# Two-block float32 kernel: scalar_tensor_tensor for tensor_tensor, attention band on TensorE, softmax scaling on ScalarE

## The chip, the core and the metric

The kernel runs on one core of a Trainium2 chip. The metric is the device time of one execution in microseconds (us). The engines are TensorE (PE in the profile; PEld is its weight load), VectorE (DVE), ScalarE (ACT), GpSimd (POOL) and SyncE (SP, which issues most loads). Each engine takes its instructions in order and waits at the first one whose input is not there.

## The reference

One sequence of 512 tokens with 1024 features passes two blocks in float32, each of depth 2. The first block mixes retention and a gated linear recurrence and has a gated feed-forward part. In the second block, each of its two layers (l = 0, 1) runs a sliding-window attention and a delta-rule recurrence (rwkv7) side by side, joins them, and has a feed-forward part with a convolution. What the change touches most is the attention, 16 query heads in 4 groups, 4 blocks of 128 queries:

```python
s = jnp.einsum('bnhqgd,...') * 64 ** -0.5
s = jnp.where(mask, s, -jnp.inf)          # band: 0 <= distance < 128
m = jnp.maximum(jnp.max(s, -1, keepdims=True), sink)
pr = jnp.exp(s - m)
pr = pr / (jnp.sum(pr, -1, keepdims=True) + jnp.exp(sink - m))
```

and, in the recurrence, the keys' factor `k = k * (1.0 + (iclr - 1.0) * k_a)`.

## The kernel before

Every large product is made of three fast matmuls (`mm_k`, L303 to L305): weights and activations are each split into a rounded high part and a rest, and high by high, high by rest and rest by high are added in PSUM. The high part is a copy on ScalarE (L287 for weights, L277 for activations), and the rest is a subtraction of two SBUF tiles on VectorE (L288, L278); in the stage below the weights' rest runs on GpSimd instead (`lo_eng`). Other work uses plain float32 matmuls.

`mixer2` is the stage around the change; it occurs once in each of the two layers. Generators for the recurrence's keys (`rw_a`, `rw_solve`) and for the attention (`attention`) are woven together by estimated costs, and the tile framework then orders each engine's instructions. The keys run alone at first (one pair of heads out of four), then beside the attention. From `rw_a` this text needs: `ic` comes from ScalarE, `t` is `ic` times one column plus another (L1141, VectorE), `k` is multiplied by `t` on GpSimd (L1142), `bk` takes products on VectorE (L1146, L1147), and 8 matmuls read `bk` (L1157). `rw_solve` is a chain of 62 small VectorE instructions (L1185, L1186). `rope2` rotates a projection out of PSUM with five VectorE instructions (L943, L946) and one addition on GpSimd (L947).

An attention item is one group and one block of queries: 16 items in a layer, of which 12 see 256 keys (wide) and 4 see 128 (narrow). `att_scores` makes an item's scores: four float32 matmuls with 64 rows (QK, L983) into two PSUM banks, `sc` for the two heads with e = 0 and `mg` for those with e = 1, one buffer each. e = 0 reads partitions 0 to 63 and e = 1 partitions 64 to 127. For each bank VectorE adds the band mask while copying to SBUF (L988) and takes the maximum (L989); three tiny instructions (L991 to L993) bring in the sink; ScalarE takes four exponentials with their sums (L996); VectorE divides (L998, L999) and scales the four heads (L1001). `att_values` transposes the result two items later (L1012, L1014) and multiplies by the values (L1023).

## Time and profile before

| what | us |
|---|---|
| three runs, median (lowest to highest) | 4038.07 (4033.7 to 4040.94) |
| the profiled execution | 4036.65 |
| its span, first to last instruction | 4034.8 |
| TensorE busy in it (modelled ends) | 3762.3 (93%) |
| VectorE busy | 2667.9 (66%) |
| ScalarE busy | 1774.9 (44%) |
| GpSimd busy | 576.6 (14%) |

The profiled execution lies 1.4 us below the median. Matmuls overlap in the pipeline and their ends are modelled, so a share of busy time near 100% does not say that TensorE runs at its peak; how close two matmuls start to each other says more. [...]

### The profile page before, as it was taken

Reading aid. Unit: us, or ns where it says so; the run is one execution under the profiler, and the core shown is the slowest. Engines: PE = TensorE matmul, PEld = TensorE weight load, DVE = VectorE, ACT = ScalarE, POOL = GpSimd, SP = SyncE. Lnnn points to the kernel's source line nnn. Section 1 sums busy time; section 2 is a strip of 40 time slices with the busy share of each in tenths; the row PEclk is TensorE's granted clock in tenths of the full one; section 3 lists DMA queues with packets and bytes.
Section 4 is the critical chain, followed back from the end, with each engine's and each line's share of the span. In section 5 each row is a group of like instructions: output and inputs, shape, how many; then the busy total and the mean of one; then the engine's idle time right before and its main releaser. Section 6 shows DMA issues by size and latency. Waiting matters only on the chain.

```text
span 4034.8 us, 56574 instructions
## 1 busy us (share of the span) xinstructions
PE 3762.3 (93%) x19888; PEld 3117.2 (77%) x19888; DVE 2667.9 (66%) x5595; ACT 1774.9 (44%) x3727; POOL 576.6 (14%) x515
## 2 busy tenths in 40 slices
PE   7998999999999988889999999998888989999998
PEld 6877888888888876657778888896665777888887
DVE  7888444555644567887664676687788775476667
ACT  4433333544433352435553554455344555354444
POOL 0201000110100033222110200014331220020001
PEclk9999999999999998989999999999888999999999
DMA  8466333312333343343227433344334323743334
GB/s 287 153 204 189 97 94 95 94 48 63 100 95 96 91 147 105 97 128 109 91 65 255 124 107 92 99 153 152 96 98 130 110 81 101 234 126 97 94 96 137
DMA packets 316573, 487.34 MB, mean 121 GB/s; under 512 B 79744, under 2 KB 127744, under 8 KB 316160
## 3 DMA queue, kind: packets, MB, share of 16 engines
q1 hardware_dynamic: 240256, 422.82, 34.0%
q10 hardware_dynamic: 76032, 60.90, 4.7%
q8 instruction: 157, 2.57, 0.3%
q14 instruction: 128, 1.05, 0.1%
HBM read 422.72 MB, written 60.88 MB: 120 GB/s over the span
## 4 chain that ended last, share of the span: by engine, by line
PE 55%; DVE 13%; ACT 3%; issue 3%; POOL 1%; DMA 1%; ACTq 0%; SPq 0%; POOLq 0%; DVEq 0%
PE ps L303 15%; PE ps L304 15%; PE ps L305 15%; DVE tm L1185 2%; PE ps L1317 1%; DVE tt L1186 1%; PE ps L1300 1%; PE ps L1157 1%; DVE ro L946 1%; DVE wl L288 1%; PE ps L983 1%; ACT wh L287 1%; PE ps L1023 1%; PE ps L1280 1%; PE ps L1285 1%
## 5 line engine op out<-in xcount | busy, mean ns | idle before, releaser
L303 PE MATMUL ps<-hi,wh 128*128 128x512 f32 (+1 forms) x4384 | 1635.3, 374 | 41.5 <-DVE ro L946 18.1
L305 PE MATMUL ps<-hi,wl 128*128 128x512 f32 (+1 forms) x4384 | 1622.1, 371 | 9.7 <-DVE wl L288 5.2
L304 PE MATMUL ps<-lo,wh 128*128 128x512 f32 (+1 forms) x4384 | 1622.7, 371 | 7.8 <-DVE lo L449 4.6
L287 ACT ACTIVATE wh<-raw 128x512 fp32r<-128x512 f32 (+1 forms) x1158 | 710.1, 620 | 1281.8 <-PE ps L304 1065.7
L288 DVE TENSOR_TENSOR wl<-raw,wh 128x512 fp32r<-128x512 f32 (+1 forms) x1005 | 690.8, 693 | 515.9 <-ACT wh L287 487.1
L303 PEld LDWEIGHTS ps<-hi,wh 128*128 128x128 f32 x4384 | 840.6, 192 | 181.3 <-issue 19.6
L305 PEld LDWEIGHTS ps<-hi,wl 128*128 128x128 f32 x4384 | 841.4, 192 | 143.7 <-DVE wl L288 7.8
L304 PEld LDWEIGHTS ps<-lo,wh 128*128 128x128 f32 x4384 | 842.5, 192 | 138.4 <-DVE lo L449 4.9
L288 POOL TENSOR_TENSOR wl<-raw,wh 128x512 fp32r<-128x512 f32 (+1 forms) x153 | 200.1, 1318 | 1193.2 <-ACT wh L287 1165.2
L1381 POOL TENSOR_TENSOR x<-x,ys 128x256 f32<-128x256 f32 x48 | 43.6, 909 | 862.9 <-DVE ys L1380 793.0
L482 DVE SCALAR_TENSOR_TENSOR ad<-ad,cact 128x1024 f32<-128x1024 f32 x96 | 116.7, 1220 | 29.2 <-DMA ad<-in_ada 29.1
L175 DVE TENSOR_TENSOR acc<-acc,sq 128x256 f32<-128x256 f32 (+1 forms) x175 | 96.1, 552 | 25.2 <-ACT sq L174 23.1
L1157 PE MATMUL ps<-bk,adg 128*128 128x192 f32 x256 | 67.2, 384 | 46.5 <-DVE bk L1147 20.5
L1319 DVE COPY sv<-ps 64x64 f32<-64x64 f32 x224 | 49.5, 221 | 90.4 <-PE ps L1317 87.6
L1185 DVE TENSOR_TENSOR tm<-lu,tt 128x126 f32<-128x126 f32 (+22 forms) x248 | 100.1, 404 | 9.0 <-DMA lu<-ls 4.0
L1580 DVE TENSOR_TENSOR u<-ps,r 128x512 f32<-128x512 f32 x88 | 60.5, 690 | 67.7 <-PE ps L305 67.0
L1317 PEld LDWEIGHTS ps<-sv,add 128*128 128x128 f32 (+1 forms) x512 | 77.9, 189 | 31.9 <-issue 8.8
L1292 POOL TENSOR_SCALAR add<-rdg 64x512 f32<-64x512 f32 x32 | 51.5, 1609 | 351.3 <-DVE add L1301 226.6
L1157 PEld LDWEIGHTS ps<-bk,adg 128*128 128x128 f32 x256 | 47.3, 216 | 64.8 <-issue 34.2
L1317 PE MATMUL ps<-sv,add 128*128 128x64 f32 (+1 forms) x512 | 91.1, 272 | 3.7 <-DVE sv L1319 2.3
L1320 ACT ACTIVATE y<-ps 64x64 f32<-64x64 f32 x256 | 54.7, 216 | 88.7 <-DVE sv L1319 49.5
L1186 DVE TENSOR_TENSOR tt<-tt,tm 128x126 f32<-128x126 f32 (+22 forms) x248 | 80.7, 325 | 3.7
(356 smaller groups left out, 5168.7 us busy)
## 6 DMA issues: line engine op xcount, KB each, us to landing
raw<-in_q_win SPq DMA_DIRECT2D x224, 256.0 KB, 2.9
ad<-in_ada SPq DMA_DIRECT2D x96, 512.0 KB, 4.4
raw<-in_q_w_up SPq DMA_DIRECT2D x184, 256.0 KB, 2.7
raw<-in_win SPq DMA_DIRECT2D x98, 256.0 KB, 3.1
raw<-in_w_val SPq DMA_DIRECT2D x92, 256.0 KB, 2.6
raw<-in_w_gate SPq DMA_DIRECT2D x92, 256.0 KB, 2.8
raw<-in_q_w_down SPq DMA_DIRECT2D x74, 256.0 KB, 2.6
raw<-in_w_down SPq DMA_DIRECT2D x64, 256.0 KB, 2.6
```

What stands on the lines that cost most here:

```text
L175: nc.vector.tensor_tensor(out=self.acc[:, cs], in0=self.acc[:, cs], in1=q, op=ADD)
L287: nc.scalar.activation(h, raw, AF.Copy)
L288: self.lo_eng.tensor_tensor(out=l, in0=raw, in1=h.bitcast(F32), op=SUB)
L303: nc.tensor.matmul(o, h, ah, start=k == first, stop=False)
L304: nc.tensor.matmul(o, h, al, start=False, stop=False)
L305: nc.tensor.matmul(o, l, ah, start=False, stop=k == last)
L482: nc.vector.scalar_tensor_tensor(out=raw, in0=raw, scalar=1.0, in1=self.cact, op0=MUL, op1=MUL, accum_out=m)
L1157: nc.tensor.matmul(o, ad[:, c], bk[:, c], start=True, stop=True)
L1185: nc.vector.tensor_tensor(out=t, in0=lc, in1=tt[:, 0:c, j:j + 1].to_broadcast([P, c, n]), op=MUL)
L1186: nc.vector.tensor_tensor(out=tt[:, 0:c, j + 1:32], in0=tt[:, 0:c, j + 1:32], in1=t, op=ADD)
L1317: nc.tensor.matmul(o, add[h][rows, c], c3(sv[h])[rows, c], start=True, stop=True)
L1580: nc.vector.tensor_tensor(out=u, in0=pj(ff), in1=r2, op=MUL)
```

## The change

1. In about twenty places, a `tensor_tensor` on VectorE with both inputs in SBUF becomes a `scalar_tensor_tensor` that first multiplies by the constant 1.0. Shapes, operands and engine stay. Places on GpSimd and places that read PSUM keep their form.
2. In `att_scores` the mask is no longer added on VectorE. Each QK matmul is preceded by one of identity (128 rows) by band into the same PSUM region, and accumulates on top. The maximum is read from PSUM, the exponentials read PSUM and write the SBUF tile, and the tiny instructions go from three to two.
3. The four scalings of an item move from VectorE to ScalarE.
4. In `rw_a`, `t` moves from VectorE to ScalarE.
5. Once per layer, band and identity are rounded into the matmul's format and the negated sinks are made (three small VectorE instructions).

```diff
@@ weights
-        self.lo_eng.tensor_tensor(out=l, in0=raw, in1=h.bitcast(F32), op=SUB)
+        if self.lo_eng is nc.vector:
+            nc.vector.scalar_tensor_tensor(out=l, in0=raw, scalar=1.0, in1=h.bitcast(F32), op0=MUL, op1=SUB)
+        else:
+            nc.gpsimd.tensor_tensor(out=l, in0=raw, in1=h.bitcast(F32), op=SUB)
...
@@ rope_tables
-        self.band = self.at.tile([P, 256], F32, name=self.name("band"), tag="band")
-        nc.sync.dma_start(self.band, self.I["band"])
+        t = self.T("bd")[:, :256]
+        nc.sync.dma_start(t, self.I["band"])
+        self.band = self.at.tile([P, 256], F32R, name=self.name("band"), tag="band")
+        nc.vector.tensor_copy(self.band, t)
+        self.identr = self.at.tile([P, P], F32R, name=self.name("identr"), tag="identr")
+        nc.vector.tensor_copy(self.identr, self.ident)
...
@@ att_scores
-                hs = slice(64 * e, 64 * e + 64)
-                nc.tensor.matmul(p[:, j * 256:j * 256 + nk], qs[j][hs, n * P:n * P + P], self.kd[g][hs, k0:k0 + nk], start=True, stop=True)
+                hs, o = slice(64 * e, 64 * e + 64), p[:, j * 256:j * 256 + nk]
+                nc.tensor.matmul(o, self.identr, self.band[:, 256 - nk:256], start=True, stop=False)
+                nc.tensor.matmul(o, qs[j][hs, n * P:n * P + P], self.kd[g][hs, k0:k0 + nk], start=False, stop=True)
         for e, p in enumerate(ps):
-            t = self.at.tile([P, S], F32, name=self.name("sc"), tag="sc", bufs=5)
-            v2 = lambda a: a.rearrange("p (e k) -> p e k", e=2)[:, :, 0:nk]
-            bd = self.band[:, 256 - nk:256].rearrange("p (o k) -> p o k", o=1).to_broadcast([P, 2, nk])
-            nc.vector.tensor_tensor(out=v2(t), in0=v2(p), in1=bd, op=ADD)
-            nc.vector.tensor_reduce(out=mx[:, e:4:2], in_=v2(t), axis=AX.X, op=MAX)
-            sc.append(t)
-        nc.vector.tensor_tensor(out=mx, in0=mx, in1=sink, op=MAX)
-        nc.vector.tensor_scalar(out=nm, in0=mx, scalar1=-1.0, scalar2=None, op0=MUL)
-        nc.vector.tensor_tensor(out=es, in0=sink, in1=mx, op=SUB)
+            nc.vector.tensor_reduce(out=mx[:, e:4:2], in_=v2(p), axis=AX.X, op=MAX)
+            sc.append(self.at.tile([P, S], F32, name=self.name("sc"), tag="sc", bufs=5))
+        nc.vector.scalar_tensor_tensor(out=nm, in0=mx, scalar=-1.0, in1=self.nsink[:, 4 * g:4 * g + 4], op0=MUL, op1=ALU.min)
+        nc.vector.scalar_tensor_tensor(out=es, in0=sink, scalar=1.0, in1=nm, op0=MUL, op1=ADD)
...
         for hd in range(4):
-            nc.scalar.activation(view(hd), view(hd), AF.Exp, bias=nm[:, hd:hd + 1], accum_out=sm[:, hd:hd + 1])
+            nc.scalar.activation(view(hd), ps[hd % 2][:, (hd // 2) * 256:(hd // 2) * 256 + nk], AF.Exp, bias=nm[:, hd:hd + 1], accum_out=sm[:, hd:hd + 1])
...
         for hd in range(4):
-            nc.vector.tensor_scalar(out=view(hd), in0=view(hd), scalar1=sm[:, hd:hd + 1], scalar2=None, op0=MUL)
+            nc.scalar.activation(view(hd), view(hd), AF.Copy, scale=sm[:, hd:hd + 1])
...
@@ rw_a
-        nc.vector.tensor_scalar(out=t, in0=ic, scalar1=self.hka[l][:, i:i + 1], scalar2=self.oka[l][:, i:i + 1], op0=MUL, op1=ADD)
+        nc.scalar.activation(t, ic, AF.Identity, bias=self.oka[l][:, i:i + 1], scale=self.hka[l][:, i:i + 1])
...
@@ rw_solve
-            nc.vector.tensor_tensor(out=t, in0=lc, in1=tt[:, 0:c, j:j + 1].to_broadcast([P, c, n]), op=MUL)
-            nc.vector.tensor_tensor(out=tt[:, 0:c, j + 1:32], in0=tt[:, 0:c, j + 1:32], in1=t, op=ADD)
+            nc.vector.scalar_tensor_tensor(out=t, in0=lc, scalar=1.0, in1=tt[:, 0:c, j:j + 1].to_broadcast([P, c, n]), op0=MUL, op1=MUL)
+            nc.vector.scalar_tensor_tensor(out=tt[:, 0:c, j + 1:32], in0=tt[:, 0:c, j + 1:32], scalar=1.0, in1=t, op0=MUL, op1=ADD)
```

Outside `mixer2` the order of every engine is the same before and after. Inside it the framework orders anew. Lines of the changed kernel stand some 10 to 17 lower in its file: QK is L1001 there, the band's matmul L1000, the exponential L1009, the scaling L1014, `t` L1154, the projections L313 to L315.

TensorE, first layer, the first wide item (`ps_13959` is its bank `sc`, `ps_13960` its bank `mg`, `kd` the keys, `ro` the rotated queries; L1157 and L305 are the keys' and a projection's matmuls). Before:

```order
6791 L983 MATMUL ps_13959<-kd_13594,ro_13747 128x256
6792 L983 MATMUL ps_13960<-kd_13594,ro_13747 128x256
6793 L983 MATMUL ps_13959<-kd_13594,ro_13792 128x256
6794 L983 MATMUL ps_13960<-kd_13594,ro_13792 128x256
6795 L1157 MATMUL ps_14034<-bk_13139,adg 128x192
```

And in the changed kernel:

```order
6791 L1000 MATMUL ps_13966<-band_13528,identr_13530 128x256
6792 L1001 MATMUL ps_13966<-kd_13600,ro_13753 128x256
6793 L1000 MATMUL ps_13967<-band_13528,identr_13530 128x256
6794 L1001 MATMUL ps_13967<-kd_13600,ro_13753 128x256
6795 L1000 MATMUL ps_13966<-band_13528,identr_13530 128x256
6796 L1001 MATMUL ps_13966<-kd_13600,ro_13798 128x256
6797 L1000 MATMUL ps_13967<-band_13528,identr_13530 128x256
6798 L1001 MATMUL ps_13967<-kd_13600,ro_13798 128x256
```

Two QK matmuls on different partitions no longer stand next to each other; a matmul of 128 rows stands between any two.

ScalarE, the same item: exponentials, a weight's high part (`wh`), and what follows. Before:

```order
1101 L996 ACTIVATE sc_13965,am_13956<-sc_13965,am_13957 128x256
1102 L996 ACTIVATE sc_13968,am_13956<-sc_13968,am_13957 128x256
1103 L996 ACTIVATE sc_13965,am_13956<-sc_13965,am_13957 128x256
1104 L996 ACTIVATE sc_13968,am_13956<-sc_13968,am_13957 128x256
1105 L997 ACTIVATE am_13958<-am_13958 128x4
1106 L287 ACTIVATE wh_14272<-raw_14271 128x512
```

And in the changed kernel:

```order
1108 L1009 ACTIVATE sc_13977,am_13963<-ps_13966,am_13964 128x256
1109 L1009 ACTIVATE sc_13979,am_13963<-ps_13967,am_13964 128x256
1110 L1009 ACTIVATE sc_13977,am_13963<-ps_13966,am_13964 128x256
1111 L1009 ACTIVATE sc_13979,am_13963<-ps_13967,am_13964 128x256
1112 L1010 ACTIVATE am_13965<-am_13965 128x4
1113 L294 ACTIVATE wh_14265<-raw_14264 128x512
1114 L1014 ACTIVATE sc_13977<-sc_13977,am_13963 128x256
1115 L1014 ACTIVATE sc_13979<-sc_13979,am_13963 128x256
1116 L1014 ACTIVATE sc_13977<-sc_13977,am_13963 128x256
1117 L1014 ACTIVATE sc_13979<-sc_13979,am_13963 128x256
1118 L294 ACTIVATE wh_14283<-raw_14282 128x512
```

The exponentials now read the banks, and four scalings stand ahead of the next weight's high part.

TensorE at the third head's keys in the first layer, shortly before the attention's first item (L1133 gives the keys' norms, L1157 needs `bk`, L303 to L305 are projections). Before:

```order
6718 L1133 MATMUL ps_13934<-c_hsel,sq_13841 128x64 x4
6719 L1157 MATMUL ps_14029<-bk_13139,adg 128x192
6720 L303 MATMUL ps_14085<-hi_12302,wh_14105 128x512
6721 L304 MATMUL ps_14085<-lo_12303,wh_14105 128x512
6722 L305 MATMUL ps_14085<-hi_12302,wl_14106 128x512
6723 L303 MATMUL ps_13755<-hi_12288,wh_13757 128x512
```

And in the changed kernel (L1146 is the norms, L1170 the matmul that needs `bk`):

```order
6718 L1146 MATMUL ps_13941<-c_hsel,sq_13848 128x64 x4
6719 L315 MATMUL ps_14095<-hi_12300,wl_14116 128x512
6720 L313 MATMUL ps_14095<-hi_12302,wh_14115 128x512
6721 L314 MATMUL ps_14095<-lo_12303,wh_14115 128x512
6722 L315 MATMUL ps_14095<-hi_12302,wl_14116 128x512
6723 L313 MATMUL ps_13761<-hi_12288,wh_13763 128x512
...
6750 L1000 MATMUL ps_13811<-band_13528,identr_13530 128x128
6751 L1170 MATMUL ps_14038<-bk_13139,adg 128x192
```

The first matmul that needs `bk` stands behind a whole projection now, not ahead of it.

## Rows read from the trace of the kernel before

**Rows 1.** the page's parts 1 and 2: busy us (share of the span) xinstructions; 40 slices

```profile
PE 3762.3 (93%) x19888; PEld 3117.2 (77%) x19888; DVE 2667.9 (66%) x5595; ACT 1774.9 (44%) x3727; POOL 576.6 (14%) x515
DVE  7888444555644567887664676687788775476667
PEclk9999999999999998989999999999888999999999
```

**Rows 2.** by stretch: us, PE, PEld, DVE, ACT, POOL busy (x), clock, DMA, GB/s

```profile
1445.00:1586.00 141.00, 112.15 (x607) 93.39 (x606) 93.28 (x201) 53.94 (x99) 61.12 (x52) 0.93 0.44 137
1586.00:1692.00 106.00, 96.35 (x466) 69.13 (x464) 85.17 (x237) 43.84 (x138) 33.39 (x28) 0.92 0.30 90
1692.00:1798.00 106.00, 88.91 (x409) 60.65 (x407) 88.16 (x265) 42.76 (x127) 17.08 (x14) 0.86 0.34 101
2989.00:3095.00 106.00, 88.98 (x409) 60.72 (x407) 88.40 (x264) 42.46 (x126) 16.97 (x14) 0.86 0.34 101
```

**Rows 3.** groups, VectorE, 1586 to 1798: xcount, busy us, mean ns, idle before

```profile
L988 DVE TENSOR_TENSOR sc<-ps,band 128x512 f32<-128x512 f32 (+1 forms) x32 | 19.6, 617 | 5.2 <-PE ps L1012 3.5 <-PE ps L983 1.5
L1001 DVE TENSOR_SCALAR sc<-sc,am 128x256 f32<-128x256 f32 (+1 forms) x64 | 19.5, 343 | 0.1
L1141 DVE TENSOR_SCALAR t<-ic,om,om 128x512 f32<-128x512 f32 x5 | 5.6, 1113 | 0.0
```

**Rows 4.** in order of time, TensorE: start us, us, instructions in a row

```profile
1725.85 1.05 PE L983 MATMUL ps<-kd,ro 64*128 64x128 f32 x8
1726.83 0.92 PE L1157 MATMUL ps<-bk,adg 128*128 128x192 f32 x4
...
1736.61 1.13 PE L983 MATMUL ps<-kd,ro 64*128 64x256 f32 x8
1737.67 0.50 PE L304 MATMUL ps<-lo,wh 128*128 128x512 f32 x1
...
1738.24 0.40 PE L303 MATMUL ps<-hi,wh 128*128 128x512 f32 x1
1738.57 1.13 PE L983 MATMUL ps<-kd,ro 64*128 64x256 f32 x4
1739.62 0.50 PE L304 MATMUL ps<-lo,wh 128*128 128x512 f32 x1
1739.96 0.40 PE L305 MATMUL ps<-hi,wl 128*128 128x512 f32 x1
1740.20 0.40 PE L303 MATMUL ps<-hi,wh 128*128 128x512 f32 x1
```

**Rows 5.** groups, ScalarE, 1586 to 1798

```profile
L996 ACT ACTIVATE sc<-sc,am 128x256 f32<-128x256 f32 (+1 forms) x64 | 30.0, 470 | 21.3 <-DVE am L992 20.5 <-issue 0.8
```

**Rows 6.** the chain that ended last, 1692 to 1798, shares by line

```profile
by line: DVE tm L1185 10.2%; DVE tt L1186 8.4%; PE ps L1023 7.6%; PE ps L1157 7.4%; PE ps L983 7.1%; PE ps L1012 5.5%; DVE ro L946 5.2%; DVE sc L988 3.8%; DVE am L989 3.4%; PE ps L1121 3.0%; issue 2.8%; DVE x L1158 2.6%; PE ps L304 2.6%; PE
```

**Rows 7.** in order of time, 1565 to 1580: TensorE, then VectorE

```profile
1571.73 0.98 PE L1157 MATMUL ps<-bk,adg 128*128 128x192 f32 x2 [5.33 <-DVE bk L1147]
1578.75 0.77 PE L303 MATMUL ps<-hi,wh 128*128 128x512 f32 x1 [4.76 <-DVE ro L946]
1566.52 0.54 DVE L1141 TENSOR_SCALAR t<-ic,om,om 128x512 f32<-128x512 f32 x1
1570.91 0.68 DVE L1147 TENSOR_TENSOR bk<-zs,wi 128x512 f32<-128x512 f32 x1
1572.86 0.68 DVE L943 TENSOR_TENSOR ro<-ps,cos 128x512 f32<-128x512 f32 x1
```

**Rows 8.** groups by shape, VectorE, whole span

```profile
L288 DVE TENSOR_TENSOR wl<-raw,wh 128x512 fp32r<-128x512 f32 x924 | 646.7, 706 | 508.0 <-ACT wh L287 479.2 <-PE ps L304 12.7 <-DMA raw<-in_q_win 4.1
L1583 DVE TENSOR_TENSOR cv<-cv,cv 128x512 f32<-128x512 f32 x44 | 30.4, 690 | 1.2
```

**Rows 9.** single lines, VectorE: duration ns min/median/max, first and last start

```profile
L1146 DVE SCALAR_TENSOR_TENSOR bk<-ic,wi x16: 635/684/1742, 1515.3 to 3083.8; 128x512 f32<-128x512 f32 x16
L1147 DVE TENSOR_TENSOR bk<-zs,wi x16: 636/678/1761, 1513.0 to 3084.7; 128x512 f32<-128x512 f32 x16
```

More of the change, by code (lines that the diff above doesn't have):

```diff
@@ L269, in load_const, with add_to @@
         return t
+    def add_to(self, pool, out, a, b, op):
+        nc = self.nc
+        if pool:
+            nc.gpsimd.tensor_tensor(out=out, in0=a, in1=b, op=op)
+        else:
+            nc.vector.scalar_tensor_tensor(out=out, in0=a, scalar=1.0, in1=b, op0=MUL, op1=op)
     def split(self, src, T=None):
@@ L277, in split @@
         nc.scalar.activation(h, src, AF.Copy)
-        nc.vector.tensor_tensor(out=l, in0=src, in1=h.bitcast(F32), op=SUB)
+        nc.vector.scalar_tensor_tensor(out=l, in0=src, scalar=1.0, in1=h.bitcast(F32), op0=MUL, op1=SUB)
         return h, l
@@ L448, in put_split @@
             nc.scalar.activation(h, t, AF.Copy)
[L449 removed]
+            self.add_to(k % 2, l, t, h.bitcast(F32), SUB)
         else:
@@ L1332, in rw_seq @@
         rs = self.rsqrt(vr)
-        nc.vector.tensor_tensor(out=c3(y), in0=c3(y), in1=b8(rs), op=MUL)
+        nc.vector.scalar_tensor_tensor(out=c3(y), in0=c3(y), scalar=1.0, in1=b8(rs), op0=MUL, op1=MUL)
         yield 0.0, 6.0
@@ L1634, in evac @@
             y = ys[m][:, cs]
-            nc.vector.tensor_tensor(out=y, in0=y, in1=g, op=MUL)
+            nc.vector.scalar_tensor_tensor(out=y, in0=y, scalar=1.0, in1=g, op0=MUL, op1=MUL)
             n1.add(y, cs)
```

25 lines of the change are left out of this document (14 added, 11 removed).

## Prediction

> **What bounds the kernel now.** The page comes first: over the span TensorE is busy 93%, VectorE 66%, ScalarE 44%, and VectorE's slices lie at 7 or more in the places where TensorE's granted clock dips under 9 tenths [rows 1]. So most of the kernel is bound by TensorE, and work taken from VectorE there is worth nothing. The exception is the stage `mixer2`, which occurs twice; the second time its stretches read like the first within 1 us. Second view, the stretches [rows 2]. 1586 to 1692 (call it B) and 1692 to 1798 (C) hold the 16 attention items of layer 0: nine in B (six wide, three narrow), seven in C (six wide, one narrow). In B TensorE is busy 96 of 106 us and VectorE 85; in C both are at 88 or 89. Neither engine alone is the bound; they hand work to each other and lose time both ways. TensorE loses twice: it idles 9.7 us in B and 17.1 in C, and it runs partly at the lower level, which at a mean granted clock of 0.92 and 0.86 is worth 8.5 us in B and 15 in C. Counted at the full clock its work is therefore 88 us in B and 74 in C. Third view, the chain in C: the largest shares are VectorE's solve chain and TensorE's attention and key matmuls, none over about a tenth [rows 6]. 1445 to 1586 (A) is the keys alone; its end is paced by VectorE [rows 2, 7].
>
> I sum against the profiled execution, 4036.65 us, which is 1.4 below the median of the three runs. About 0.2%, 8 us, is what a measurement here can tell from no change.
>
> **Part 1, the form of the instruction.** The nearest rows for a two-input instruction in SBUF with 512 columns are 690 ns as a tensor_tensor [rows 8] and, on one tile and next to each other, a median of 684 as a scalar_tensor_tensor with a constant and 678 as a tensor_tensor [rows 9]. Between 12 ns saved and 6 ns lost on each of the 924 weights' rests is 11 us of VectorE time to the good or 6 to the bad, and nearly all of them lie where TensorE is the bound. I take 0, and keep a few us for the range.
>
> **Part 2, what VectorE loses.** Per layer, in B and C: 32 additions of the band, 19.6 us, 64 scalings, 19.5, and five `t`, 5.6 [rows 3]. Spread over the items that is about 25 us in B and 19 in C, so VectorE falls from 85 to 60 and from 88 to 69. The maximum reads PSUM now; the band's addition did so too at 617 ns on average [rows 3], so it keeps its price. The three small instructions per layer of part 5 of the change are under 2 us together and stand beside projections.
>
> **Part 3, what TensorE gains.** Four QK matmuls of a wide item that alternate between the two halves of the partitions take 1736.61 to 1737.67, 1.06 us; two of one half alone take 1738.57 to 1739.62, 1.05 us: neighbours on different halves run at the same time, and the same work unpaired takes twice as long [rows 4]. Around the lone two, the projections are late as well: from L303 at 1738.24 to L305 at 1739.96 are 1.72 us, of which two projections at 0.24 (the next step, to 1740.20) are 0.48. So two QK cost 1.24, of which some 0.19 is the way in and out of the 64-row form. If as much again hides inside the 1.05, one bare QK is 0.43. With the band's matmul (256 columns, half of 0.24) between any two, none runs beside another, and each QK pays its own way in and out: 4 x (0.43 + 0.19 to 0.38 + 0.12) is 3.0 to 3.7, and I take 3.5, since the isolated pair is the nearest row. Before, an item costs 1.25 where it stands paired and 2.5 where its banks come free apart; in the order before, about half stand each way, so 1.9. A narrow item goes from 1.2 (0.98 as a row, plus the way in) to 2.6 by the same steps. Per layer: 12 x 1.6 + 4 x 1.4 = 25 us more for TensorE, 14 in B and 11 in C. Without any cost of switching it would be 12 x 0.3 = 4; if all had been paired before, 12 x 2.4 + 4 x 1.7 = 36.
>
> [...]
>
> **Part 4, what ScalarE gains.** 64 scalings per layer; the nearest row is the exponential of the same tiles, 470 ns, so 30 us, and five `t` at under 1 us each [rows 5]. ScalarE goes from 44 to about 61 in B and from 43 to about 59 in C [rows 2]. That is covered by 40 us of idle time in each, unless its order holds something up: the scalings wait for VectorE's reciprocal, and behind them stand weights' high parts, which GpSimd and then TensorE wait for. I cost it at 0; without that cover, one VectorE instruction's wait of 0.7 us per item would be 11 us a layer.
>
> **Part 5, the end of A.** TensorE waits 5.33 us for `bk`, runs three projections, and waits 4.76 us for a rotation to give its bank back [rows 7]. In the new order the matmul that needs `bk` stands a projection later, so the first wait goes; but the rotation begins only at 1572.86 behind `t` (0.54) and `bk` (0.68), and that bank is what is late next. `t` leaves VectorE and L1147 moves behind the rotation, and some POOL conflict with them: I take 3 us, between 1 (the two instructions) and 10 (both waits).
>
> **The sum.** TensorE's work at full clock becomes 88 + 14 = 102 in B and 74 + 11 = 85 in C. What it loses in B (9.7 + 8.5 = 18) and C (17 + 15 = 32) comes mostly from waiting on VectorE. With VectorE's share down by a quarter, I keep half: 102 + 9 = 111 in B (5 longer than 106) and 85 + 16 = 101 in C (5 shorter). With A, 3 us less per layer, 6 in all: 4036.65 - 6 = 4031 us. That is no change that can be told, a little on the fast side.
>
> **Rivals.**
> *VectorE was the pace.* If only a quarter of the losses stays, B is 106.5 and C 93, and with A each layer gains 15.5 us: 4036.65 - 31 = 4006. For it: C's chain, where VectorE's lines hold the first places [rows 6], and both waits of [rows 7]. Against it: B, where TensorE is at 96 of 106. 0.26.
>
> *The banks are held too long* (slower). Before, a bank comes free after one addition on VectorE of 617 ns [rows 3]; after, only when the exponentials have read it: two maxima, the small ones, and three or four exponentials at 470, about 4 us after the last QK. There is one buffer per bank, so the next item's QK waits in TensorE's order, and with it everything behind. It decides where fewer than about 4 us of other matmuls stand between two items; in the new order that is so for some six items per layer, in C above all. At 2.6 us (the four exponentials and their sums' reads) that is 12 x 2.6 = 31 us: 4031 + 31 = 4062. For it: ScalarE already sat idle 20.5 us for the sinks' result ahead of the exponentials [rows 5]. Against it: 16 items share 212 us, 13 each. 0.27.
>
> *TensorE gains the work and gives nothing back.* All losses stay: B 120, C 117, with A 22 us per layer: 4081. Against it: the losses are waits on an engine that gets lighter. 0.08.
>
> *The new form escapes GpSimd.* Held up by GpSimd, a tensor_tensor takes up to 1761 ns, and the weights' rests average 706 where an undisturbed group has 690 [rows 8, 9]. If the new form were never held, 924 x 16 ns = 15 us come off VectorE: 4031 - 15 = 4016 at best. Against it: the scalar_tensor_tensor with a constant took up to 1742 in the same place [rows 9]. 0.03. [...]
>
> **How the numbers follow.** The forecast itself has 0.36. Its own spread, from TensorE's 4 to 36 us per layer and A's 1 to 10, is about 12 us to each side of 4031: 4019 to 4043. Two fifths of that lie more than 8 us under 4036.65, and nothing more than 8 above it. Faster by over 0.2%: 0.26 + 0.03 + 0.4 x 0.36 = 0.43. Within: 0.6 x 0.36 = 0.22. Slower: 0.27 + 0.08 = 0.35. The range reaches from 4002, the first rival with a few us more, to 4064, the banks with a few more; it leaves out the 0.08 and the ends of the others.
>
> **What the profile of the changed kernel would show.** Part 1: the weights' rests at 690 to 710 ns on average. Part 2: VectorE near 60 and 69 us in the two stretches. Part 3: from one QK to the next in an item 0.7 to 0.95 us, and the attention's matmuls no longer in pairs; below 0.6 the lower end holds. Part 4: ScalarE near 60 us per stretch, and little idle time ahead of L1014. Part 5: the wait ahead of the first L1170 of the third head gone. The bank rival would show as TensorE idle ahead of L1000 or L1001 with the exponential, L1009, as what ended it. Wrong altogether would be a change outside the two `mixer2` stages.

## The result and the profile after

The changed kernel took 4091.13 us (median of four runs, 4089.23 to 4093.79) where the kernel before took 4038.59 (four runs): a ratio of 1.0129, 95% interval 1.0116 to 1.0142, so 52 us more. The forecast was 4031 with a range up to 4064. It missed, and on the other side.

The first view is the page again, parts 1 and 2, in the form of [rows 1]:

```profile
PE 3826.8 (94%) x20016; PEld 3157.1 (77%) x20016; DVE 2612.5 (64%) x5361; ACT 1829.3 (45%) x3871; POOL 577.9 (14%) x515
DVE  7888444564644566657664676686666766476667
PEclk9999999999999998989999999998898999999999
```

VectorE lost 55 us of work, ScalarE gained 54, TensorE is busy 64.5 us longer. VectorE's slices fell where `mixer2` runs; the dips of the clock did not go with them.

Where in the program is the time? ScalarE rounds each weights' panel (L287, L294 after), 1158 times in both kernels and in the same sequence, so the k-th of them is a mark in both traces. The 451st stands 1.2 us later after the change, the 571st 31.1, the 811th 30.1, the 946th 55.0, and from there to the end the distance changes by about 1 us. So the loss is made in the two pieces from 451 to 571 and from 811 to 946, the two `mixer2` stages. I divide each at the first score matmul (L983 before, L1001 after) and the last value matmul (L1023, L1036): the keys alone, the attention's stretch, and what follows. First before, then after, in the columns of [rows 2], layer 0:

```profile
1438.00:1586.50 148.50, 119.65 (x642) 99.45 (x640) 100.75 (x218) 58.24 (x110) 67.00 (x58) 0.93 0.45 140
1586.50:1784.10 197.60, 175.12 (x827) 122.38 (x826) 165.70 (x475) 85.32 (x261) 49.60 (x42) 0.88 0.30 91
1784.10:2164.30 380.20, 347.40 (x2003) 277.59 (x2000) 249.32 (x567) 184.48 (x462) 66.19 (x52) 0.98 0.39 123
```

```profile
1439.20:1590.90 151.70, 119.21 (x642) 99.65 (x640) 103.07 (x214) 60.58 (x113) 65.21 (x58) 0.91 0.44 137
1590.90:1808.50 217.60, 201.41 (x884) 136.63 (x883) 134.09 (x368) 109.30 (x328) 49.53 (x42) 0.89 0.27 80
1808.50:2195.40 386.90, 354.94 (x2010) 284.32 (x2007) 253.05 (x561) 185.66 (x465) 67.75 (x52) 0.96 0.38 122
```

How to read them: length less PE busy is TensorE's idle time. The clock column is the mean of TensorE's granted clock as a share of full speed; the records of the two traces, before and after, give it as 1.0 or 0.5 and nothing between, and from one projection of 512 columns to the next are 0.227 us (median) at 1.0 and 0.427 at 0.5, in both. PE busy times (1 - clock) is therefore an estimate of what the lower level cost (the clock is printed to two places, so this is good to about 1 us in the middle row and 2 in the last). In the attention's stretch of layer 0 TensorE's idle time fell only from 22.5 to 16.2 us, its losses to the clock stayed (21.0 and 22.2), and its work at full clock rose by 25. That is 20 us longer, although VectorE has 31.6 us less to do there. Keys alone: 3.2 longer. Behind: 6.7 longer, about what the clock's loss grew by (0.98 to 0.96, 7 us). In the second layer the three are 7.6, 14.2 and 3.2 longer. Over both stages, with the clock unrounded, the changed kernel is 54.8 us longer: TensorE's work at full clock is 46.9 more, its loss to the clock 16.1 more and its idle time 8.2 less.

What TensorE does for the scores, in order of time, as in [rows 4]:

```profile
1644.43 0.40 PE L315 MATMUL ps<-hi,wl 128*128 128x512 f32 x1
1644.66 0.28 PE L1000 MATMUL ps<-band,identr 128*128 128x256 f32 x1
1644.88 0.70 PE L1001 MATMUL ps<-kd,ro 64*128 64x256 f32 x2
1645.50 0.38 PE L1000 MATMUL ps<-band,identr 128*128 128x256 f32 x1
1645.81 0.70 PE L1001 MATMUL ps<-kd,ro 64*128 64x256 f32 x2
1646.44 0.38 PE L1000 MATMUL ps<-band,identr 128*128 128x256 f32 x1
...
1648.32 0.65 PE L1036 MATMUL ps<-pt,vt 128*64 128x256 f32 x4
```

From start to start, a band matmul inside the group takes 0.31 us and a score 0.63 (one score leaves two records, hence x2). The item takes 1644.66 to 1648.32, 3.66 us. Summed over a layer and taken from start to start, idle time left out, the score and band matmuls take 58.0 us of TensorE where the scores took 27.5.

TensorE's waits in layer 0 (1439 to 2195; us in total, times, longest) and two groups of ScalarE's and one of VectorE's in the attention's stretch (the counterparts of [rows 3] and [rows 5]):

```profile
PE ps L313 <- DVE ro L960: 17.6, 4, 12.1
PE ps L1170 <- DVE bk L1159: 10.3, 3, 5.9
PE ps L1000 <- ACT sc L1009: 4.0, 2, 2.0
PE ps L1170 <- DVE bk L1160: 1.3, 2, 1.0
```

```profile
L1014 ACT ACTIVATE sc<-sc,am 128x256 f32<-128x256 f32 (+1 forms) x64 | 25.8, 473 | 20.5 <-DVE am L1012 20.5
L1154 ACT ACTIVATE t<-ic,om,om 128x512 f32<-128x512 f32 x5 | 4.1, 815 | 4.5 <-DMA od<-ao 4.5
L1003 DVE TENSOR_REDUCE am<-ps 128x2 f32<-128x512 f32 (+1 forms) x32 | 19.6, 620 | 26.1 <-PE ps L1001 25.8
```

TensorE waits for the banks (L1000, ended by the exponential L1009) only 4 us. ScalarE stands 20.5 us in front of the scalings for VectorE's reciprocal, where I had expected little. VectorE now sits idle 26 us in front of the maxima for TensorE's scores: there it has become the engine that waits.

### The profile page after: what moved, and what is told of

The parts are those of the page before. It is cut to its first block, busy times and chain, and to the rows that moved or that the text cites. A ratio compares the mean times of both kernels' runs of the same rounds, so it can differ in the third digit from the quotient of the medians.

```text
span 4089.3 us, 56798 instructions
## 1 busy us (share of the span) xinstructions
PE 3826.8 (94%) x20016; PEld 3157.1 (77%) x20016; DVE 2612.5 (64%) x5361; ACT 1829.3 (45%) x3871; POOL 577.9 (14%) x515
## 5 line engine op out<-in xcount | busy, mean ns | idle before, releaser
L313 PE MATMUL ps<-hi,wh 128*128 128x512 f32 (+1 forms) x4384 | 1636.4, 375 | 49.7 <-DVE ro L960 33.2
L315 PE MATMUL ps<-hi,wl 128*128 128x512 f32 (+1 forms) x4384 | 1626.7, 372 | 10.7 <-DVE wl L296 5.8
L294 ACT ACTIVATE wh<-raw 128x512 fp32r<-128x512 f32 (+1 forms) x1158 | 708.8, 620 | 1257.8 <-PE ps L314 1030.9
L296 DVE SCALAR_TENSOR_TENSOR wl<-raw,wh 128x512 fp32r<-128x512 f32 (+1 forms) x1005 | 689.6, 692 | 505.5 <-ACT wh L294 478.6
L313 PEld LDWEIGHTS ps<-hi,wh 128*128 128x128 f32 x4384 | 843.7, 193 | 187.2 <-issue 34.5
L315 PEld LDWEIGHTS ps<-hi,wl 128*128 128x128 f32 x4384 | 841.6, 192 | 147.0 <-POOL wl L298 9.2
L1198 DVE SCALAR_TENSOR_TENSOR tm<-lu,tt 128x126 f32<-128x126 f32 (+22 forms) x248 | 101.9, 411 | 12.7 <-DMA lu<-ls 5.1
L175 DVE SCALAR_TENSOR_TENSOR acc<-acc,sq 128x256 f32<-128x256 f32 (+1 forms) x175 | 95.3, 548 | 22.5 <-ACT sq L174 20.4
L1009 ACT ACTIVATE sc<-ps,am 128x256 f32<-128x256 f32 (+1 forms) x128 | 55.5, 445 | 79.8 <-DVE am L1005 76.3
L1170 PE MATMUL ps<-bk,adg 128*128 128x192 f32 x256 | 68.4, 382 | 24.2 <-DVE bk L1159 19.3
L1199 DVE SCALAR_TENSOR_TENSOR tt<-tt,tm 128x126 f32<-128x126 f32 (+22 forms) x248 | 85.1, 343 | 5.5
```

The source lines that it names most:

```text
L175: nc.vector.scalar_tensor_tensor(out=self.acc[:, cs], in0=self.acc[:, cs], scalar=1.0, in1=q, op0=MUL, op1=ADD)
L294: nc.scalar.activation(h, raw, AF.Copy)
L296: nc.vector.scalar_tensor_tensor(out=l, in0=raw, scalar=1.0, in1=h.bitcast(F32), op0=MUL, op1=SUB)
L313: nc.tensor.matmul(o, h, ah, start=k == first, stop=False)
L315: nc.tensor.matmul(o, l, ah, start=False, stop=k == last)
L1170: nc.tensor.matmul(o, ad[:, c], bk[:, c], start=True, stop=True)
```

## The experiments

All runs stand in one table: median, difference to the kernel before on the same chip, 95% interval of the ratio, and by how much the three stretches of the profiled execution (both layers together) are longer than in that of the kernel before (keys alone 296.5 us, attention 395.1, behind 806.7). The difference is of medians and the ratio of means; the profiled execution can lie some us off its median (e2's 7 below it, e12's 6 above). The order in which each engine's instructions stand is made anew for every kernel, and no run held it fixed; so a difference of some 10 us in one stretch may be the order alone. The runs tell apart what is larger, or what comes back in both layers.

| run | median us | difference | ratio, interval | keys | attention | behind |
|---|---|---|---|---|---|---|
| the change | 4091.1 | +52.5 | 1.0116 to 1.0142 | +10.8 | +34.1 | +9.9 |
| e1 change, band on VectorE | 4064.1 | +27.1 | 1.0051 to 1.0084 | +10.0 | +27.5 | -6.9 |
| e2 band on TensorE alone | 4068.1 | +31.0 | 1.0057 to 1.0102 | +3.2 | +7.9 | +19.4 |
| e3 scalings and t on ScalarE alone | 4067.7 | +30.7 | 1.0060 to 1.0090 | +9.1 | +22.8 | -7.0 |
| e4 form of the instruction alone | 4035.8 | -1.3 | 0.9987 to 1.0006 | +2.9 | -2.1 | -0.7 |
| e5 t alone | 4042.7 | +5.9 | 1.0007 to 1.0026 | +9.4 | +4.5 | -3.6 |
| e6 scalings alone | 4056.0 | +19.2 | 1.0037 to 1.0067 | +1.1 | +25.5 | -9.9 |
| e7 change, bands first | 4044.3 | +7.5 | 1.0010 to 1.0030 | +4.3 | +0.9 | +1.6 |
| e8 band alone, bands first | 4039.2 | +2.4 | 0.9999 to 1.0018 | -0.5 | -0.4 | +2.4 |
| e9 as e6, constant factor | 4052.7 | +15.0 | 1.0020 to 1.0046 | +7.9 | +17.4 | -5.6 |
| e10 as e2, scores in pairs | 4042.8 | +5.0 | 1.0007 to 1.0027 | +0.2 | +11.8 | -4.9 |
| e11 as e2, no band at all | 4024.3 | -13.4 | 0.9948 to 0.9977 | -0.4 | -7.8 | -7.4 |
| e12 loose ScalarE work | 4047.2 | +10.4 | 1.0015 to 1.0034 | +16.3 | -2.3 | -0.2 |
| e13 fused add and maximum | 4030.9 | -5.9 | 0.9977 to 1.0009 | +0.1 | -13.1 | +2.3 |
| e14 two scalings of four | 4044.1 | +7.3 | 1.0004 to 1.0023 | +2.8 | +10.1 | -8.2 |
| e15 tied ScalarE work | 4068.2 | +29.4 | 1.0060 to 1.0089 | +3.0 | +31.1 | -1.2 |
| e16 as e13, minimum | 4047.9 | +9.1 | 1.0015 to 1.0035 | +0.8 | -2.0 | +15.5 |
| e17 e13 again | 4035.5 | -3.4 | 0.9990 to 1.0015 | +2.7 | -5.6 | +0.2 |

### The change in its parts: e1 to e6

The first theory (T): TensorE's added time is the whole loss, and VectorE's relief is worth nothing.

e1, the changed kernel with the band's addition put back to VectorE (maximum and Exp from SBUF and the three small operations come back with it; the lines here are the band's alone):

```diff
-                nc.tensor.matmul(o, self.identr, self.band[:, 256 - nk:256], start=True, stop=False)
+            nc.vector.tensor_tensor(out=v2(t), in0=v2(p), in1=bd, op=ADD)
```

> The changed kernel with the band added by VectorE as before (all its other parts kept). Theory T (TensorE's occupied time goes straight to the end: the score lines take 39.0 + 19.5 us of it per layer where they took 27.5, and the work taken off VectorE gave back 3.5 us of idle): without the band all of the loss goes, 4028 to 4042 us. Rival S (the four scalings, now on ScalarE, lengthen each item): 4055 to 4075. Rival V (the work taken off VectorE is worth what I forecast, some 14 us a layer, and the band hid it): 4005 to 4025.

e2, the kernel before with that one part of the change (maximum and Exp from PSUM and the two small operations come with it; the lines here are the band's alone):

```diff
+                nc.tensor.matmul(o, self.identr, self.band[:, 256 - nk:256], start=True, stop=False)
-            nc.vector.tensor_tensor(out=v2(t), in0=v2(p), in1=bd, op=ADD)
```

> The kernel before with the band on TensorE alone (scalings, the factor t and tensor_tensor stay on VectorE as before). T: 4085 to 4105, the whole loss or more. S: 4055 to 4075, a part of the loss. V: 4060 to 4080, since VectorE's relief of 1.2 us an item would show here too.

e3, the kernel before with

```diff
-            nc.vector.tensor_scalar(out=view(hd), in0=view(hd), scalar1=sm[:, hd:hd + 1], ...
+            nc.scalar.activation(view(hd), view(hd), AF.Copy, scale=sm[:, hd:hd + 1])
-        nc.vector.tensor_scalar(out=t, in0=ic, scalar1=self.hka[l][:, i:i + 1], ...
+        nc.scalar.activation(t, ic, AF.Identity, bias=self.oka[l][:, i:i + 1], scale=self.hka[l][:, i:i + 1])
```

> The kernel before with the four scalings of an item and the factor t on ScalarE alone. T: 4028 to 4042. S: 4050 to 4070. V: 4010 to 4028, as VectorE is relieved of 12 us a layer.

e4, the kernel before with `scalar_tensor_tensor` by 1.0 for `tensor_tensor` in the places of the change, such as

```diff
-        nc.vector.tensor_tensor(out=l, in0=src, in1=h.bitcast(F32), op=SUB)
+        nc.vector.scalar_tensor_tensor(out=l, in0=src, scalar=1.0, in1=h.bitcast(F32), op0=MUL, op1=SUB)
```

> The kernel before with tensor_tensor as scalar_tensor_tensor in VectorE's some twenty places alone. T, S, V: all 4034 to 4042, nothing; if the form takes longer beside GpSimd it would be 4045 or more.

T fell at once, and of the three theories S alone stayed within its bounds in all of e1, e2 and e3. The form costs nothing (e4, as all expected). But the band alone makes only 31 of the 52 us (e2), and without it 27 stay (e1), which is what the two moves to ScalarE cost by themselves (e3, 30.7). Both halves of the change lose about the same. e5 and e6 split the second half: e5 has e3's second pair of lines alone, e6 its first.

> The kernel before with only the keys' factor t on ScalarE. Theory Q (ScalarE's queue stands still in front of each item's scalings, 27.5 us a layer for VectorE's reciprocal, and the copies that TensorE waits for stand behind): t has little part in it, 4040 to 4048 (the keys' stage alone grew by 3 us a layer). Rival K (t itself lengthens the keys' chain, since it takes 815 ns on ScalarE and waits its turn there): 4055 to 4068, the whole of the 31 us.

> The kernel before with only the four scalings of an item on ScalarE. Q: 4055 to 4065, the larger part of the 31 us. K: 4035 to 4045, nothing.

t costs 6, the scalings 19: the scalings are the larger part. And t sits in the keys' stretch (+9.4 in both layers together), the scalings in the attention's (+25.5, of which 9.9 are less work left behind).

Where the band's 31 us lie surprised me. The three stretches of e2, layer 0:

```profile
1434.40:1584.70 150.30, 122.05 (x646) 101.29 (x644) 103.61 (x222) 59.14 (x110) 65.94 (x58) 0.92 0.43 139
1584.70:1782.90 198.20, 188.74 (x881) 131.08 (x882) 149.76 (x430) 81.82 (x258) 47.81 (x39) 0.94 0.29 89
1782.90:2173.10 390.20, 357.53 (x2009) 284.85 (x2006) 253.15 (x562) 186.48 (x465) 70.38 (x54) 0.96 0.37 120
```

In layer 0 the attention's stretch is as long as before (198.2 against 197.6). TensorE works 23 us more at full clock, and its idle time (22.5 to 9.5) and its losses to the clock (21.0 to 11.3) give back just that: 43.5 to 20.8, half, as I had assumed. In the second layer less comes back (43.5 to 26), and the stretch is 7.2 longer. Most of the loss is behind the attention: 10 us longer in layer 0, 9 in the second. One thing to be seen there is that the keys, which share TensorE with the attention, fell behind although the attention did not. The last step of the last solve, in VectorE's order of time, before and in e2:

```profile
1844.98 0.58 DVE L1186 TENSOR_TENSOR tt<-tt,tm 128x16 f32<-128x16 f32 x1
```

```profile
1866.00 0.18 DVE L1189 TENSOR_TENSOR tt<-tt,tm 128x16 f32<-128x16 f32 x1
```

It ends 20.6 us later, and what follows in the stage is built on it. By itself that need not cost: from the attention's end to the end of this step are 61 us before, 83 in e2 and 76 in e15 (below), and e15's third stretch is no longer than before. The other is the clock: 15.8 of the 19.4 us behind the attention, both layers together, are its loss. In one place of e2 it falls:

```profile
1842.00:1862.00 20.00, 17.31 (x69) 14.01 (x68) 12.94 (x40) 4.15 (x10) 0.13 (x1) 0.66 0.41 139
```

With levels of 1.0 and 0.5, a mean of 0.66 is the lower one for two thirds of these 20 us (from 1849 to 1855 the clock was 0.50). TensorE had idled 2.7 us (1842.5 to 1845.2) as this stretch began.

### What the band costs on TensorE: e7, e8, e10, e11

e7 is the changed kernel, e8 the kernel of e2, with

```diff
+        for e, p in enumerate(ps):
+            bd = self.band[:, 256 - nk:256].rearrange("p (o k) -> p o k", o=1).to_broadcast([P, 2, nk])
+            nc.tensor.matmul(v2(p), self.identr, bd, start=True, stop=False)
         for j in range(2):
             for e, p in enumerate(ps):
-                nc.tensor.matmul(o, self.identr, self.band[:, 256 - nk:256], start=True, stop=False)
-                nc.tensor.matmul(o, qs[j][hs, n * P:n * P + P], self.kd[g][hs, k0:k0 + nk], start=False, stop=True)
+                nc.tensor.matmul(o, qs[j][hs, n * P:n * P + P], self.kd[g][hs, k0:k0 + nk], start=False, stop=j == 1)
```

> The changed kernel with one band matmul per bank (both halves at once) ahead of the item's four scores, which follow one another as before. Theory T (the score lines' TensorE time goes to the end as far as the attention's stretch is TensorE's): they fall from 58.5 to some 38 us a layer, so 20 us a layer less at most: 4050 to 4075. Rival (with the scalings on ScalarE the stretch waits for those, and the time saved turns to idle): 4080 to 4092.

> The kernel before with the band on TensorE alone, one matmul per bank ahead of the four scores; scalings and t stay on VectorE. T: up to 20 us a layer less than with the band between the scores (4068): 4025 to 4045. Rival P (in that kernel the attention's stretch was no longer than before, and the loss lies behind it, 8 us a layer of half clock and 3 us of TensorE's work in the stage that follows): the gain in the stretch is small and the loss behind it stays, 4050 to 4068.

e7's loss is 45 us less than the change's, e8's 29 less than e2's: e7 below T's bounds, e8 inside them. The same sums are formed in another sequence, with two band matmuls of 512 columns for four of 256, and 45 of the change's 52 us go: the largest single effect of these runs. TensorE's order of time in e7:

```profile
1601.52 0.61 PE L999 MATMUL ps<-band,identr 128*128 128x512 f32 x2
1602.07 1.14 PE L1003 MATMUL ps<-kd,ro 64*128 64x256 f32 x8
1603.13 0.92 PE L1172 MATMUL ps<-bk,adg 128*128 128x192 f32 x4
```

Both bands take 0.55 us, the four scores 1.06: 1.61 for what took 3.66. Per layer the score and band matmuls take 31.8 us in e7 and 37.7 in e8 (27.5 before). e10 keeps four band matmuls and only pairs the scores (both bands of a half, then both scores; `os2` holds the half's regions in the two banks):

```diff
         for j in range(2):
+            for o in os2:
+                nc.tensor.matmul(o, self.identr, self.band[:, 256 - nk:256], start=True, stop=False)
             for e, o in enumerate(os2):
-                nc.tensor.matmul(o, self.identr, self.band[:, 256 - nk:256], start=True, stop=False)
```

> The kernel before with the band on TensorE alone, four band matmuls as in the change, but both of a half's bands first and then both of its scores, so that two scores follow one another on different halves of the rows. Theory A (what costs is that no two scores are neighbours): the score lines fall from 54 to some 42 us a layer, 4042 to 4052. Rival M (each band matmul and each change of form costs): 4058 to 4068, as with the bands between the scores.

```profile
1649.51 0.53 PE L990 MATMUL ps<-band,identr 128*128 128x256 f32 x2
1649.97 0.70 PE L993 MATMUL ps<-kd,ro 64*128 64x256 f32 x4
1650.61 1.08 PE L1028 MATMUL ps<-pt,vt 128*64 128x256 f32 x8
```

Two neighbours on different halves of the rows take 0.64 us, one alone 0.63 (in the change): the second costs nothing that shows. By the kernel's time theory A holds: 26 of e2's 31 us go when the scores are neighbours again. By the place it is less plain. Of the 27 us a layer that the score and band matmuls take more in e2 (54.5 for 27.5), the bands themselves are 18 and the scores 9; e10 (44.5) has 16 and 1, so pairing gives back 10 us a layer for the same eight matmuls an item. And e10's attention is no shorter than e2's (+11.8 and +7.9): what it gained lies behind the attention (-4.9 and +19.4). How 10 us a layer there become 26 in all, no run tells.

e11 has no band matmul at all, to see what VectorE's relief is worth when nobody pays for it:

```diff
-                nc.tensor.matmul(o, self.identr, self.band[:, 256 - nk:256], start=True, stop=False)
-                nc.tensor.matmul(o, qs[j][hs, n * P:n * P + P], self.kd[g][hs, k0:k0 + nk], start=False, stop=True)
+                nc.tensor.matmul(o, qs[j][hs, n * P:n * P + P], self.kd[g][hs, k0:k0 + nk], start=True, stop=True)
```

> The kernel before with its attention as in the change (reduction and Exp from PSUM, two small operations for three) but with no band added at all, so the mask is left out: what VectorE's relief of 20 us a layer is worth when TensorE pays nothing for it. Theory P (VectorE's relief is worth little in itself): 4022 to 4038. Rival V (as I forecast, the band's removal from VectorE shortens the stretch by half of TensorE's losses there, some 25 us a layer): 3985 to 4012.

13 us for both layers, where 39 us of additions left VectorE (19.6 a layer, [rows 3]), and up to 11 of the 13 may be TensorE's own: more of the scores stand paired, 21.8 us a layer for 27.5. So the relief is worth a third of its length at most, and theory P held. By this estimate TensorE may pay no more than 6 to 7 us a layer for it. e8 pays 10 (37.7 less 27.5) and is no faster than before; the change pays 30.

### What the scalings cost on ScalarE: e9, e12, e14, e15

In e6 ScalarE stands 30 us a layer in front of the scalings (L1001). e9 takes that wait away by a constant factor in place of the softmax's:

```diff
-            nc.scalar.activation(view(hd), view(hd), AF.Copy, scale=sm[:, hd:hd + 1])
+            nc.scalar.activation(view(hd), view(hd), AF.Copy, scale=0.125)
```

> As the run with only the four scalings on ScalarE (4056), but each scales by the constant 0.125 in place of the softmax's factor, so that it doesn't wait for VectorE's reciprocal; the normalisation is left out. Theory Q (the wait at the head of ScalarE's queue costs, 30 us of it in one layer's attention): 4034 to 4044, the 19 us go. Rival D (what costs is ScalarE's own 64 x 0.40 us a layer): 4050 to 4060, nothing changes.

The two kernels' groups, e6 first:

```profile
L1001 ACT ACTIVATE sc<-sc,am 128x256 f32<-128x256 f32 (+1 forms) x64 | 25.6, 471 | 30.3 <-DVE am L999 30.1 <-DVE tt L1186 0.2
```

```profile
L1001 ACT ACTIVATE sc<-sc 128x256 f32<-128x256 f32 (+1 forms) x64 | 19.5, 377 | 0.0
```

The wait went from 30.3 us to nothing, and the kernel gained some 4 of 19 us (the two intervals overlap). The wait is a small part of the price at most. I then added ScalarE work that nobody needs, with the scalings left on VectorE:

```diff
             nc.scalar.activation(view(hd), view(hd), AF.Exp, bias=nm[:, hd:hd + 1], accum_out=sm[:, hd:hd + 1])
+            nc.scalar.activation(<scratch>[:, :nk], self.band[:, :nk], AF.Copy, scale=0.125)
```

> The kernel before with four more ScalarE instructions per item of the size of a scaling, from a constant tile into a scratch tile that nobody reads; the scalings stay on VectorE. Theory D (ScalarE's own time: everything behind it in its in-order queue, the keys' factors and the copies that TensorE waits for, comes later): 4050 to 4062. Rival L (the scalings' own dependants, the transposes, are what comes later): 4034 to 4043.

This missed its place: with nothing to wait for, these instructions ran in the keys' stretch (ScalarE busy there 76 us where it was 58 in layer 0; 85 in the attention's, as before), which became 16 us longer, both layers together. The kernel's 10 us more lie between the bounds of D and L. But no item's chain holds these instructions, and TensorE's idle time among the keys rose from 28.9 to 34.3 us in layer 0 (32.7 to 34.0 in the second): ScalarE's time costs there too, with no item's chain to pass it on. e15 gives each the item's bias as an operand, so that it runs behind the item's Exp:

```diff
+            nc.scalar.activation(<scratch>[:, :nk], self.band[:, :nk], AF.Identity, bias=nm[:, hd:hd + 1])
```

> The kernel before with four more ScalarE instructions per item of the size of a scaling, into a scratch tile that nobody reads, each with the item's bias as an operand, so that it runs behind the item's Exp; the scalings stay on VectorE. D (ScalarE's own time in the attention): 4048 to 4060, the attention's stretch 206 to 212 us a layer where it was 198. L (what depends on the scalings is what comes later): 4034 to 4044, the stretch as before.

```profile
L997 ACT ACTIVATE du<-band,am 128x256 f32<-128x256 f32 (+1 forms) x64 | 30.0, 468 | 0.0
```

```profile
1588.80:1800.40 211.60, 184.61 (x834) 128.04 (x833) 165.82 (x480) 107.61 (x324) 47.78 (x40) 0.87 0.28 85
```

ScalarE's 30 us a layer, without one wait of their own and with no reader, make the attention's stretch 14 and 17 us longer and the kernel 29, more than D's bounds. So ScalarE's own time in its queue is a price, 29 us for 60 us of it, although the engine is busy only 108 of 212 us. One thing e15 does not keep apart: each added instruction stands behind one of the item's four Exps, so from one Exp to the next are 0.89 us (1658.64 to 1659.53) where there were 0.49 (1663.90 to 1664.39 before), and the item's own softmax comes later too. In e12 it did not.

How the time reaches TensorE shows in part. Its waits that ScalarE ended rose from 3.8 to 8.9 us in each layer, those that VectorE ended stayed (18.0 before; 17.1 and 18.0). Layer 0, before and then e15:

```profile
PE ps L1023 <- ACT pt L1014: 3.8, 2, 3.5
```

```profile
PE ps L1024 <- ACT pt L1015: 6.9, 4, 3.6
PE ps L303 <- ACT du L997: 2.0, 1, 2.0
```

Over both `mixer2` stages, with the clock unrounded, e15's 33 us are 5 of idle time, 23 of loss to the clock and 6 of work; e6's 17 are 7, 10 and 0. So in both most of the price appears as a lower clock. Why 5 us more of idle time go with 23 us more lost to the clock, no run tells.

e14 leaves two of the four scalings on VectorE:

```diff
+            if hd < 2:
+                nc.scalar.activation(view(hd), view(hd), AF.Copy, scale=sm[:, hd:hd + 1])
+            else:
                 nc.vector.tensor_scalar(out=view(hd), in0=view(hd), scalar1=sm[:, hd:hd + 1], ...
```

> The kernel before with two of the four scalings of an item on ScalarE. D, in proportion: 4043 to 4050. A threshold (ScalarE has room for two): 4032 to 4040.

7.3 us of 19.2: nearer to proportion than to a threshold.

### In search of a version that beats both: e13, e16, e17

e11 points to relief that costs neither TensorE nor ScalarE. e13 is the kernel before with addition and maximum in one VectorE instruction per head:

```diff
-            nc.vector.tensor_tensor(out=v2(t), in0=v2(p), in1=bd, op=ADD)
-            nc.vector.tensor_reduce(out=mx[:, e:4:2], in_=v2(t), axis=AX.X, op=MAX)
+            for j in range(2):
+                nc.vector.tensor_tensor_reduce(out=t[:, c], in0=p[:, c], in1=self.band[:, 256 - nk:256], scale=1.0, scalar=sink[...], op0=ADD, op1=MAX, accum_out=mx[...])
-        nc.vector.tensor_tensor(out=mx, in0=mx, in1=sink, op=MAX)
```

> The kernel before with the band's addition and the maximum in one VectorE instruction per head (four of 256 for two additions and two reductions of 512, and the maximum with the sink in it); nothing goes to TensorE or ScalarE. Theory P (VectorE's relief is worth what the run without a band shows, 13 us for about 20 us a layer): with about half of that relief 4024 to 4036. Rival: the four instructions take as long as the four before, 4034 to 4045.

```profile
L990 DVE CUSTOM_DVE_ANT_0 sc<-ps,band,vec 128x256 f32<-128x256 f32 (+1 forms) x64 | 26.9, 444 | 11.8 <-PE ps L1012 7.5 <-PE ps L983 4.2
L990 DVE DVE_READ_ACCUMULATOR2_ANT am<- 128x1 f32 x64 | 5.2, 82 | 0.0
```

32 us a layer where addition and reduction took 39. Ten runs went from 4024 to 4051. e17 is the same kernel again; e16 a form with one small operation fewer (scores negated by the keys' factor, the band positive, minimum in place of maximum):

```diff
-                    nc.scalar.activation(t[64 * f:64 * f + 64], kr[64 * e:64 * e + 64], AF.Copy, scale=0.125)
+                    nc.scalar.activation(t[64 * f:64 * f + 64], kr[64 * e:64 * e + 64], AF.Copy, scale=-0.125)
-        nc.vector.tensor_scalar(out=nm, in0=mx, scalar1=-1.0, scalar2=None, op0=MUL)
```

> e13 again, for its interval: 4026 to 4036 if the gain is there, as its attention's stretches were 191 us where they were 198; 4034 to 4044 if it was scatter.

> As e13, with the scores negated by the keys' factor, so that the fused instruction takes the minimum and gives Exp's bias directly: one small VectorE operation fewer in the chain of each item. If VectorE's relief in the attention's chain pays: 4020 to 4032; if e13's gain was scatter: 4034 to 4044.

The gain was not to be told from none (e17, twelve runs from 4027 to 4054, its median inside both bounds). e16 was 9 slower, outside both; in its profile all of it lies behind the attention, where 14 us more are lost to the clock. No version that I ran is surely faster than the kernel before; e8 and e13 equal it.

e17 points at why it scatters. The same stretch of the same kernel, in layer 0 and in layer 1:

```profile
1590.70:1789.40 198.70, 173.28 (x824) 120.11 (x823) 155.16 (x520) 85.58 (x261) 49.61 (x42) 0.90 0.29 90
2888.30:3079.20 190.90, 166.17 (x822) 115.43 (x823) 155.10 (x520) 85.30 (x261) 49.50 (x42) 0.94 0.30 94
```

The same instructions but for a record or two, VectorE and ScalarE equally busy, and 7.8 us between them: TensorE's mean granted clock was 0.90 in one and 0.94 in the other (17.3 and 10.0 us lost), and its idle time is the same within 1 us. Over the twelve runs the mean clock of the whole kernel goes from 0.974 in the fastest to 0.965 in the slowest.

## Why the prediction was wrong

**Part 1 was right.** I took 0 for the form; e4 gave -1.3. The weights' rests average 704 ns (706 in [rows 8]), and the longest takes 1787 ns in both forms. Of the 924 with 512 columns, 20 took over 1 us before and 19 after, each of them while a GpSimd instruction ran, and of those with none beside them (867 and 863) none took over 695 ns. So the new form is held up like the old one:

```profile
L296 DVE SCALAR_TENSOR_TENSOR wl<-raw,wh 128x512 fp32r<-128x512 f32 x924 | 645.4, 704 | 497.4 <-ACT wh L294 470.6 <-PE ps L314 12.7 <-DMA raw<-in_q_w_o_att 4.1
```

All 1005 of them, before and then after (ns min/median/max):

```profile
L288 DVE TENSOR_TENSOR wl<-raw,wh x1005: 417/691/1787, 18.2 to 4010.4; 128x512 fp32r<-128x512 f32 x158, 128x384 fp32r<-128x384 f32 x8, 128x256 fp32r<-128x256 f32 x2
L296 DVE SCALAR_TENSOR_TENSOR wl<-raw,wh x1005: 418/690/1787, 18.1 to 4064.4; 128x512 fp32r<-128x512 f32 x158, 128x384 fp32r<-128x384 f32 x8, 128x256 fp32r<-128x256 f32 x2
```

**Part 2 was right in what leaves VectorE**: 134 us busy where it was 166, in a stretch that now holds a few more steps of the solves. The maximum kept its price, as I had said (620 ns, 608 before).

**Part 3 was right step by step, and its size a little low.** A bare score of 0.43 with its way in and out of 0.19, and the band's 0.12 with another 0.19, are 0.62 and 0.31; the rows give 0.63 and 0.31. A wide item takes 3.66 us (I took 3.5); per layer it is 30.5 us more (25, with 36 as the upper bound). That every alternation of band and score pays was my estimate from a lone pair between projections [rows 4], which showed no matmul of 128 rows between two scores. The rows of the changed kernel show it: the 256 columns of the band take 0.31 us between scores, and the 512 of a projection among its like 0.23. What I did not do with this estimate was to ask whether the change had to pay it. e7 pays 0.55 for both bands of an item.

**Part 4 is the first step that failed.** I wrote that ScalarE's 30 us a layer are "covered by 40 us of idle time in each" stretch and costed them at 0. They cost 19 us for the scalings (e6) and 6 for t (e5), 31 together (e3). I had named a possible price, the wait for the reciprocal, but bounded it at 0.7 us an item and left it out; the wait was there, 30 us a layer in e6, and it was a small part of the price at most (e9). What costs is the time itself (10 us more in e12, 29 in e15): ScalarE works through its instructions in their sequence, and what stands behind the new ones comes later, idle share or not (in e15 each next Exp by 0.40 us). In e15 the copies `pt` are seen to (3.8 to 6.9 us of TensorE's waits in layer 0); the larger part, by way of the clock, is not traced to one instruction. VectorE was the fuller engine, at 80 to 83% where ScalarE was at 40 to 41 [rows 2], and still e6 lost: 19.5 us a layer taken from VectorE were bought with 25.6 on ScalarE. e15 and e6 differ chiefly in whether VectorE is relieved as well (and in 30.0 against 25.6 us of ScalarE's), and by 10 us of time for 39 us of VectorE's.

**Part 5 had the wrong sign.** The waits of TensorE in layer 0 before, as a counterpart to those shown after:

```profile
PE ps L1157 <- DVE bk L1147: 10.2, 3, 5.3
PE ps L303 <- DVE ro L946: 9.0, 5, 4.8
PE ps L1157 <- DVE bk L1146: 5.6, 2, 3.5
```

The wait for `bk` behind L1147 went (10.2 us, 1.3 now behind L1160), but that behind L1146 grew (5.6 us, 10.3 now behind L1159), and the wait for the rotation, which I had named as late next, rose from 9.0 to 17.6 us with 12.1 in one piece. The keys' stretch grew by 3.2 and 7.6 us where I took 3 off. e5 puts this down to t: with t alone on ScalarE the keys grow as much (+9.4, and +10.8 in the change), and the wait for the rotation is 9.7 us in one piece.

**The sum is the second step that failed.** By Part 3 and the sum the band alone should have cost nothing: 25 us a layer more for TensorE, and half of 50 us of losses given back. It cost 31 us (e2). "I keep half" was right for it in layer 0 (43.5 to 20.8 us; 26 in the second layer). With the scalings on ScalarE, 38.4 and 32.7 stay: much of what VectorE's relief gave back, ScalarE took. And my sum ended with the attention: the 19 us of e2 that lie behind it, most of them the clock's, have no term in it. A smaller slip moves the sum by 1.5 us a layer: I took the clock's loss off the whole length (8.5 and 15 us); off TensorE's busy time it is 7.7 and 12.4.

**The rivals.** By its time, the nearest is the one in which TensorE gains the work and gives nothing back (4081). As a mechanism it is right in part: 38.4 of 43.5 us of losses stay in layer 0, but the band alone gave back half, and the rest came over ScalarE. It had 0.08 because I counted only what gets lighter. The banks held too long, my main case for slower, cost little: 6 us of TensorE's idle time in layer 0 end with the exponential (4 in front of L1000, 2 in front of a projection), and in e8, which holds the banks as long, the whole loss is gone. A rival for part 4, with its 60 us of ScalarE's time as a price, was missing.

**What stays open.** The parts don't add up evenly: the moves to ScalarE cost 31 us alone (e3), 21 on top of the band (the change less e2) and some 5 where the bands stand first (e7 less e8). Why they cost so little there, no run tells. Nor do the runs tell why TensorE loses 8 to 16 us to the clock behind the attention (both layers together, beyond what it lost before) in e8, the change and e2, and nothing in e6 or e13's second layer. And since the order was made anew each time, a part of each difference may be the order's.

## What to carry to other kernels

Idle share of an engine that works in sequence was no cover (ScalarE was busy 85 of 198 us, and e15's 30 us a layer made the kernel 29 longer): price moved work by what stands behind it in that engine's queue, and test it with work of the same length that nobody reads, tied to the place where it will run and not between the steps of a chain that it is meant to leave alone. Two scores on different halves of the rows took 0.64 us as neighbours and one alone 0.63, so anything put on TensorE beside such a pair goes ahead of the group, not into it (1.61 us a wide item in e7, 3.66 in the change). And the relief of VectorE, one of the engines that share the pace here, was worth a third of its length at most (13 us for 39, e11), so ask first what the other engines pay.
